# A plain column pair's last products moved behind the next pair's first job, its weights shifted by 192 bytes

## The chip, the cores and the metric

The kernel runs on one core of a Trainium2 chip. The metric is the device time of one execution in microseconds (us); lower is better. The kernel before takes 904.31 us, the median of three runs (903.77 to 905.09). Names of engines: PE is TensorE, DVE is VectorE, ACT is ScalarE, POOL is GpSimd, and SP issues most of the DMAs.

## What is computed

The reference is one layer of an encoder trunk over 512 rows of 1024 channels: a norm, a wide input projection, three mixers (pooling, differential attention, a gated recurrence), gates, an output projection, and then a SwiGLU feed-forward part with a hidden width of 2816. Only the feed-forward input is touched by the change:

```
h2 = rms_norm(x, norm2_g[l])
gu = h2 @ w_ffn_in[l]
x = x + (jax.nn.silu(gu[..., :FFN_HIDDEN]) * gu[..., FFN_HIDDEN:]) @ w_ffn_out[l]
```

All of it is float32 in and out.

## The kernel before

Every float32 operand of a large product is split into a rounded part and the rest, named `hi` and `lo` (`split_w`, L176: ACT casts `hi`, DVE subtracts to get `lo`). A product is then three terms on PE, hi by hi, hi by lo and lo by hi, added up in one PSUM bank. `cols_mm` writes such a product for 8 blocks of 128 input channels, that is 24 matmuls.

The hidden width is cut into 22 column blocks of 128 (j = 0 to 21). Each needs a gate product and an up product, and so the two blocks of weights are called a pair. Pairs 1 to 21 are computed by a Strassen-like scheme in four jobs (`ffn_pair_bodies`, L1117: `first`, `second`, `third`, `fourth`), with matmuls of 256 rows: 24, 24, 24 and 12 of them. It needs sums of weight blocks (`PairChunk.add`, L255: three DVE instructions at L259, L262 and L263, tile `sums`), splits of those (`shi` on ACT L298, `slo` on DVE L300), and sums of activation blocks (`Forms.make`, tiles `fhi` and `flo`). In `third` a DVE instruction at L1154 reads the bank of the x product (`mm`) into `g`, and `fourth` adds into the same bank, so that the first matmul of `fourth` waits for L1154.

Pair 0 is plain: `ffn_start_job` (L1087) computes pair 1's first job, then the gate product g0 of pair 0 (two halves of 256 rows, since the last rows of h2 come late), then its up product u0 with 24 matmuls of 512 rows into a bank named `rc`. After that pair 1's other three jobs follow, then pair 2's four, and so on.

PE takes its matmuls in the order in which the program writes them. The order on DVE and ACT is set by a scheduler at build time, from its own model of time, and can be pinned by `behind(...)`, which places an instruction after given others. Each engine works through its own list in order, and waits on semaphores where it needs another's result.

At j = 4 the first job ends with two matmuls of 512 rows into a bank `tp` that nobody reads. The second one's moving rows start 16 elements, 64 bytes, further than the first one's. The kernel also has paddings of 192 and 64 bytes between tiles. In the built program the h2 and form tiles start 224 bytes past a multiple of 256, and the split weights 32 bytes past one.

Of the kernel before, what the change touches and what calls it, by code (L numbers as in the profile page):

```python
# [18 lines left out]
P = 128  # L19
# [3 lines left out]
KT = D // P  # L23
# [53 lines left out]
def encoder_kernel(ctx: ExitStack, tc: tile.TileContext, x, norm1_g, w_in, pool_w, pool_scale,  # L77
# [11 lines left out]
    def mm(out_, lhsT, rhs, start, stop, chain=False):  # L89
        i = nc.tensor.matmul(out_, lhsT=lhsT, rhs=rhs, start=start, stop=stop, skip_group_check=chain)  # L90
        tc.keep_in_program_order(i)
        n = 1
        for d in rhs.shape[1:]:
            n *= d
        pipe.t += max(0.107, n * 0.0004167 + 0.002) if rhs.dtype == F32R else max(0.216, n * 0.001667 + 0.004)
# [18 lines left out]
    def bank(name, shape=(P, 512)):  # L114
        return psum.tile(list(shape), F32, name=name, bufs=2 if name == "tp" else 3)
# [46 lines left out]
    class Part:  # L162
# [9 lines left out]
        def split(self):  # L172
            self.hi, self.lo = split_w(self.view(self.chunk.raw), self.a, self.b, self.wpool, self.skip)
            self.chunk.left -= 1

    def split_w(view, a, b, wpool=None, skip=0):  # L176

        n, k = a * b, skip // 4
        hi, lo = ((wpool or wsp).tile([P, n if wpool else 1088], F32R, name=name)[:, k:k + n]
                  .rearrange("p (a b) -> p a b", a=a) for name in ("whi", "wlo"))  # L180
        nc.scalar.copy(out=hi, in_=view)  # L181
        nc.vector.tensor_tensor(out=lo, in0=view, in1=hi.bitcast(F32), op=ALU.subtract)  # L182
        return hi, lo
# [46 lines left out]
    jobs = Jobs()  # L230
# [34 lines left out]
    @contextmanager  # L265
    def behind(after):

        with ExitStack() as st:
            for i in after:
                st.enter_context(tc.issue_after(i))  # L270
            yield
# [39 lines left out]
    def pair_parts(name, src1, src2, after=(None,) * 4):  # L311
        ch = PairChunk(src1, src2)
        ch.name = name
        ch.after = after
        return [PairPart(ch, i) for i in range(4)]

    def product(ps, part, n, r, start):

        terms = [(part.hi, r[0]), (part.hi, r[1]), (part.lo, r[0])]
        for i, (w, m) in enumerate(terms):  # L320
            for k in range(KT // 2):
                mm(ps, w[:, n, k, :], m[:, k, :], start and i == 0 and k == 0,
                   i == 2 and k == KT // 2 - 1, True)
                if k % 2:
                    yield
# [73 lines left out]
    def cols_mm(ps, part, r, nk, sub=0, lo_col=0, n=512, r_lo_last=False):  # L399
        c = slice(lo_col, lo_col + n)  # L400
        ws = slice(sub * P, sub * P + P)
        terms = [(part.hi, r[0]), (part.hi, r[1]), (part.lo, r[0])]
        if r_lo_last:
            terms[1:] = terms[:0:-1]
        for i, (w, m) in enumerate(terms):
            for k in range(nk):
                mm(ps[:, c], w[:, k, ws], m[:, k, c], i == 0 and k == 0, i == 2 and k == nk - 1)
                if k % 2:
                    yield
# [51 lines left out]
    hT = (hTp.tile([P, KT, S], F32R, name="hT_hi"), hTp.tile([P, KT, S], F32R, name="hT_lo"))  # L461
# [35 lines left out]
    first = []  # L497
# [513 lines left out]
    OUT = {}  # L1011
# [49 lines left out]
    FF = {}  # L1061
    wf = w_ffn_in[0]

    def ffn_pair_evac(j, pg, pu):
        sl = FF["t"].tile([P, S], F32, name="silu")
        nc.scalar.activation(out=sl, in_=pg, func=AF.Silu)
        nc.vector.tensor_tensor(out=hid_of(j), in0=pu, in1=sl, op=ALU.mult)

    def hid_of(j):
        return FF["hid"][j // 8][:, j % 8, :]  # L1070
# [3 lines left out]
    def hid_split(half, jp):  # L1074

        if (half, jp) in hid_parts:
            return
        early = half == 0 and jp < 2
        hi, lo = ((LAST["ws"] if early else FF["hs"]).tile([P, 2, S], F32R, name=n)
                  for n in (("shi", "slo") if early else ("hhi", "hlo")))  # L1080
        j = 2 * jp
        view = FF["hid"][j // 8][:, j % 8:j % 8 + 2, :]
        nc.scalar.copy(out=hi, in_=view)
        nc.vector.tensor_tensor(out=lo, in0=view, in1=hi.bitcast(F32), op=ALU.subtract)
        hid_parts[half, jp] = hi, lo

    def ffn_start_job(p1, u0, g0):  # L1087


        yield ("e", "H1", 1.3)  # L1090
        yield from pair_bodies[1][0](p1)
        FF["first"] = [bank("mm"), bank("rc")]
        yield from cols_mm(FF["first"][0], g0, OUT["hT"], KT, 0, 0, 256)
        yield ("e", "H3", 1.3)
        yield from cols_mm(FF["first"][0], g0, OUT["hT"], KT, 0, 256, 256, True)
        yield from cols_mm(FF["first"][1], u0, OUT["hT"], KT)

    class TilePart:

# [7 lines left out]
            return True  # L1107

        def split(self):
            self.hi, self.lo = split_w(self.chunk.raw[:, self.c], KT, P)  # L1110
            self.chunk.left -= 1

    def ffn_cols(j):

        return [wf[:, o + j * P:o + (j + 1) * P].rearrange("(kt p) c -> p kt c", p=P) for o in (FFN, 0)]

    def ffn_pair_bodies(j):  # L1117
        c = {}


        def first(part):
            f = FF["forms"]
            c["x"], c["zy"] = bank("mm")[:, 0:256], bank("rc")
            c["u"] = FF["t"].tile([P, S], F32, name="u")
            yield from product(c["x"], part, 0, f.r11, True)
            nc.scalar.copy(out=c["u"][:, 0:256], in_=c["x"])
            yield from product(c["zy"][:, 0:256], part, 1, f.r21, True)


            if j == 4:  # L1130
                w = part.hi.rearrange("p n k c -> p (n k c)")
                for skip in (0, 16):
                    mm(bank("tp"), w[:, 0:P], w[:, skip:skip + 512], True, True)

        def second(part):
            f = FF["forms"]
            y = c["y"] = c["zy"][:, 256:]
            if j == 2:
                with behind(FF["s12_2"]):
                    ffn_pair_evac(0, *FF["first"])  # L1140
            c["g"] = FF["t"].tile([P, S // 2], F32, name="g2")
            yield from product(c["x"], part, 1, f.n2, False)
            nc.scalar.copy(out=c["u"][:, 256:], in_=c["x"])
            yield from product(y, part, 0, f.n1, True)
            FF["y1"] = (nc.scalar.copy(out=c["g"], in_=y).ins,)

        def third(part):
            f = FF["forms"]
            if j == 1:
                with behind(FF["forms_end"]):  # L1150
                    pairs[2][1].chunk.add()
            c["sl"] = FF["t"].tile([P, S], F32, name="silu")
            yield from product(c["x"], part, 0, f.d, False)
            on_dve = nc.vector.tensor_tensor(out=c["g"], in0=c["x"], in1=c["g"], op=ALU.add).ins  # L1154
            if j == 1:
                FF["g1"] = (on_dve,)
            nc.scalar.activation(out=c["sl"][:, 256:], in_=c["g"], func=AF.Silu, scale=-1.0)
            yield from product(c["y"], part, 1, f.r22, False)
            nc.vector.tensor_tensor(out=c["u"], in0=c["u"], in1=c["zy"], op=ALU.add)

        def fourth(part):
            f = FF["forms"]
            yield from product(c["x"], part, 0, f.n4, False)
            nc.scalar.activation(out=c["sl"][:, 0:256], in_=c["x"], func=AF.Silu, scale=-1.0)
            nc.vector.tensor_tensor(out=hid_of(j), in0=c["sl"], in1=c["u"], op=ALU.mult)
            if j == FT - 1:
                for jp in range(2):
                    hid_split(0, jp)

        return first, second, third, fourth  # L1170

    pair_bodies = {j: ffn_pair_bodies(j) for j in range(1, FT)}
    after = {1: (None, None, "forms_mid", "forms_mid"), 2: ("g1",) * 4, 3: ("s12_2",) * 4}
    pairs = {j: pair_parts(j, *ffn_cols(j), after.get(j, (None,) * 4)) for j in range(1, FT)}
    plain = PairChunk(*ffn_cols(0))
    plain.where = "pl"
    u0, g0 = TilePart(plain, 0), TilePart(plain, 1)
    jobs.add([pairs[1][0], u0, g0], ffn_start_job)
    n_out = len(jobs.jobs)
    for j in range(1, FT):  # L1180
        for i in range(0 if j > 1 else 1, 4):
# [193 lines left out]
```

## Time and profile before

| what | value |
|---|---|
| median of three runs | 904.31 us (903.77 to 905.09) |
| the profiled execution | 903.87 us, its span 902.0 us |
| mean granted TensorE clock | 0.998 |
| PE busy | 885.1 us, 98% of the span |
| DVE, ACT busy | 586.3 us (65%), 420.8 us (47%) |
| DMA | 89.00 MB, mean 99 GB/s |

The span is the time from the first to the last instruction; 1.87 us of the execution lie around it. Times inside the trace count from the span's start. In a timeline row the columns are start in us, length in us, engine, line, operation, the names written and read, the shape, and how many instructions the row merges. Matmuls overlap in the pipeline, so a matmul's length says little: the pace is the distance from one start to the next, divided by the count.

### The profile page before, as it was taken

The numbers are of one execution on the slowest core, as the hardware profiler recorded it, in microseconds if no ns is written. First come the engines' busy times: TensorE is split into PE (matmuls) and PEld (weight loads), VectorE is DVE, ScalarE is ACT, GpSimd is POOL, SyncE is SP. The second block draws the span as 40 slices with busy tenths as digits, with TensorE's granted clock in tenths as the row PEclk, the third lists the DMA queues.
The fourth block names the chain that finished last, engine by engine and source line by source line (L and its number), as shares of the span: only waits on it lengthen the run. The fifth ranks groups of instructions, "written<-read, shape, count | busy, mean of one in ns | idle before, by whom it ended". The sixth has DMA issues, their size and how long they took to land.

```text
span 902.0 us, 13155 instructions
## 1 busy us (share of the span) xinstructions
PE 885.1 (98%) x5355; PEld 782.7 (87%) x5355; DVE 586.3 (65%) x904; ACT 420.8 (47%) x652; POOL 19.4 (2%) x34
## 2 busy tenths in 40 slices
PE   6999999999999999999999999999999999999996
PEld 5989978878998888788888898999999999888885
DVE  5787566844859764644425735998888888545544
ACT  5544343424746583332223414756556556434432
POOL 2000000000000000000000001000000000000000
PEclk9999999999999999999999999999999999999999
DMA  8330113024134115422224440154434334323302
GB/s 248 105 117 24 47 48 117 24 71 135 44 94 138 48 47 188 151 94 94 94 94 140 140 118 1 48 140 123 113 94 135 100 98 137 117 70 119 108 31 94
DMA packets 106312, 89.00 MB, mean 99 GB/s; under 512 B 2686, under 2 KB 93324, under 8 KB 106124
## 3 DMA queue, kind: packets, MB, share of 16 engines
q1 hardware_dynamic: 105532, 86.59, 31.2%
q10 hardware_dynamic: 720, 1.57, 0.5%
q8 instruction: 42, 0.69, 0.3%
q14 instruction: 18, 0.15, 0.1%
HBM read 86.06 MB, written 2.10 MB: 98 GB/s over the span
## 4 chain that ended last, share of the span: by engine, by line
PE 94%; DVE 3%; DMA 1%; ACT 1%; issue 1%; POOL 0%; POOLq 0%; SPq 0%; ACTq 0%; DVEq 0%
PE mm L90 66%; PE rc L90 23%; PE tp L90 4%; PE tp L98 2%; DMA xin<-in_x_dram 1%; DVE hid L352 1%; DMA raw<-in_w_ffn_in_dram 0%; DVE flo L352 0%; DVE h_lo L451 0%; DVE wlo L182 0%; DVE slo L300 0%; DVE hrow L432 0%; PE rc L98 0%; ACT x L1218 0%; ACT hrow L426 0%
## 5 line engine op out<-in xcount | busy, mean ns | idle before, releaser
L182 DVE TENSOR_TENSOR wlo<-raw,whi 128x1024 fp32r<-128x1024 f32 (+1 forms) x146 | 166.5, 1144 | 154.9 <-PE mm L90 77.7
L181 ACT CAST whi<-raw 128x1024 fp32r<-128x1024 f32 (+1 forms) x146 | 143.5, 990 | 211.3 <-PE mm L90 126.7
L90 PE MATMUL mm<-hT_hi,whi 128*128 128x512 f32 (+1 forms) x440 | 111.8, 390 | 0.0
L90 PE MATMUL mm<-hT_hi,wlo 128*128 128x512 f32 (+1 forms) x440 | 108.1, 381 | 0.0
L90 PE MATMUL mm<-hT_lo,whi 128*128 128x512 f32 (+1 forms) x440 | 107.9, 382 | 0.0
L90 PEld LDWEIGHTS mm<-hT_hi,whi 128*128 128x128 f32 x440 | 79.2, 191 | 16.9 <-issue 2.9
L90 PEld LDWEIGHTS mm<-hT_lo,whi 128*128 128x128 f32 x440 | 79.0, 188 | 14.8
L90 PEld LDWEIGHTS mm<-hT_hi,wlo 128*128 128x128 f32 x440 | 78.9, 188 | 14.6
L300 DVE TENSOR_TENSOR slo<-sums,shi 128x1024 fp32r<-128x1024 f32 x42 | 51.1, 1218 | 0.0
L298 ACT CAST shi<-sums 128x1024 fp32r<-128x1024 f32 x42 | 44.2, 1053 | 2.2 <-DVE sums L262 1.8
L763 DVE TENSOR_TENSOR kq<-kq,pyr 128x256 f32<-128x256 f32 x56 | 21.5, 420 | 25.6 <-PE rc L90 25.5
L90 PEld LDWEIGHTS rc<-kq,kc 128*128 128x128 f32 x224 | 30.3, 191 | 2.1 <-issue 0.5
L90 PE MATMUL rc<-kq,kc 128*128 128x128 f32 x224 | 31.6, 284 | 0.0
L885 ACT ACTIVATE s<-s,mx 128x512 f32<-128x512 f32 x32 | 23.1, 721 | 15.5 <-DVE mx L883 15.4
L727 ACT COPY kc<-kq 128x512 f32<-128x512 f32 x28 | 18.6, 666 | 21.8 <-PE rc L90 15.6
L90 PE MATMUL mm<-fhi,slo 128*128 128x256 f32 x168 | 26.1, 277 | 0.5 <-DVE slo L300 0.4
L90 PE MATMUL mm<-y_hi,whi 128*128 128x512 f32 x96 | 26.4, 393 | 0.0
L90 PE MATMUL mm<-y_lo,whi 128*128 128x512 f32 x96 | 26.2, 392 | 0.0
L90 PE MATMUL mm<-fhi,shi 128*128 128x256 f32 x168 | 26.0, 277 | 0.1
L90 PE MATMUL mm<-y_hi,wlo 128*128 128x512 f32 x96 | 25.9, 390 | 0.0
L90 PE MATMUL mm<-flo,shi 128*128 128x256 f32 x168 | 25.9, 276 | 0.0
L90 PE MATMUL mm<-whi,hhi 128*128 128x512 f32 x66 | 25.7, 389 | 0.0
(254 smaller groups left out, 1787.9 us busy)
## 6 DMA issues: line engine op xcount, KB each, us to landing
raw<-in_w_ffn_in_dram SPq DMA_DIRECT2D x44, 512.0 KB, 5.3
raw<-in_w_in_dram SPq DMA_DIRECT2D x18, 1024.0 KB, 5.2
raw<-in_w_in_dram SPq DMA_DIRECT2D x24, 512.0 KB, 4.1
raw<-in_w_ffn_out_dram SPq DMA_DIRECT2D x10, 1024.0 KB, 5.1
raw<-in_w_out_dram SPq DMA_DIRECT2D x4, 1024.0 KB, 5.2
xin<-in_x_dram SPq DMA_DIRECT2D x4, 512.0 KB, 9.4
raw<-in_w_up_rec_dram SPq DMA_DIRECT2D x2, 1024.0 KB, 7.8
x<-in_x_dram SPq DMA_DIRECT2D x1, 2048.0 KB
```

What stands on the lines that cost most here:

```text
L90: i = nc.tensor.matmul(out_, lhsT=lhsT, rhs=rhs, start=start, stop=stop, skip_group_check=chain)
L98: tc.keep_in_program_order(nc.tensor.transpose(out_, in_, idn))
L181: nc.scalar.copy(out=hi, in_=view)
L182: nc.vector.tensor_tensor(out=lo, in0=view, in1=hi.bitcast(F32), op=ALU.subtract)
L298: nc.scalar.copy(out=hi, in_=view)
L300: on_dve = nc.vector.tensor_tensor(out=lo, in0=view, in1=hi.bitcast(F32), op=ALU.subtract).ins
L352: last[0] = form(**kw).ins
L727: nc.scalar.copy(out=strided(kc, 0, [[2 * n, S // (2 * n)], [n, 2], [1, n]]), in_=strided(kq, 2 * S, [[2 * n, S // (2 * n)], [S + n, 2], [ ...
L763: nc.vector.tensor_tensor(out=xv, in0=xv, in1=tv, op=ALU.mult)
L885: nc.scalar.activation(out=s, in_=s, func=AF.Exp, scale=-1.0, bias=mx[:, c:c + 1], accum_out=zz[:, i, c:c + 1])
```

## The change

There are five edits. The order of the two plain products' parts becomes g0, u0 in the job's list. u0's 24 products are cut into three terms of eight; the first two terms stay where they were, and the third (u0's `lo` part) is written at the end of pair 2's first job. One matmul that nobody reads follows it, with u0's first `lo` block as stationary part and pair 2's `hi` weights from element 16 as moving part; the two at j = 4 are gone. The split weights of both g0 and u0 lie 192 bytes further in their tiles, so that they start 224 bytes past a multiple of 256. And the three DVE instructions that add up pair 2's weight blocks are placed behind pair 1's L1154 (L1162 in the new file), no longer ahead of it.

```
-        yield from cols_mm(FF["first"][1], u0, OUT["hT"], KT)
+        yield from first_u(u0, 0)
+        yield from first_u(u0, 1)
+        FF["u0"] = u0
+
+    def first_u(u0, term):
+        w, m = (u0.lo if term == 2 else u0.hi), OUT["hT"][term % 2]
+        for k in range(KT):
+            mm(FF["first"][1], w[:, k, :], m[:, k, :], (term, k) == (0, 0), (term, k) == (2, KT - 1), True)
+            if k % 2:
+                yield
...
-            self.hi, self.lo = split_w(self.chunk.raw[:, self.c], KT, P)
+            self.hi, self.lo = split_w(self.chunk.raw[:, self.c], KT, P, None, 192)
...
-            if j == 4:
+            if j == 2:
+                yield from first_u(FF["u0"], 2)
                 w = part.hi.rearrange("p n k c -> p (n k c)")
-                for skip in (0, 16):
-                    mm(bank("tp"), w[:, 0:P], w[:, skip:skip + 512], True, True)
+                mm(bank("tp"), FF["u0"].lo[:, 0, :], w[:, 16:528], True, True)
...
-            if j == 1:
-                with behind(FF["forms_end"]):
-                    pairs[2][1].chunk.add()
...
             if j == 1:
                 FF["g1"] = (on_dve,)
+                with behind(FF["g1"]):
+                    pairs[2][1].chunk.add()
```

Where the instructions now stand is shown at three places. The numbers behind names are those of one tile; `x4` merges four instructions.

PE, around the end of pair 2's first job (tiles `mm_4994` and `rc_4995`, after the change `mm_4986` and `rc_4987`), before:

```order
L90 MATMUL rc_4995<-h2_hi_4263,whi_4961 128x256 x4
L90 MATMUL rc_4995<-h2_lo_4264,whi_4961 128x256 x4
L90 MATMUL rc_4995<-h2_hi_4263,wlo_4962 128x256 x4
L90 MATMUL mm_4994<-fhi_4866,shi_4965 128x256 x4
L90 MATMUL mm_4994<-flo_4867,shi_4965 128x256 x4
```

The same place after the change, where `rc_4760` is u0's bank and `wlo_4536` its `lo` weights:

```order
L90 MATMUL rc_4987<-h2_hi_4263,wlo_4954 128x256 x4
L90 MATMUL rc_4760<-h2_hi_4263,wlo_4536 128x512 x8
L90 MATMUL tp_5022<-whi_4953,wlo_4536 128x512
L90 MATMUL mm_4986<-fhi_4858,shi_4957 128x256 x4
L90 MATMUL mm_4986<-flo_4859,shi_4957 128x256 x4
```

Eight matmuls and one now stand between pair 2's first and second job; the eight are gone from the end of u0, ahead of pair 1's second job.

DVE, around pair 1's reading of its x bank (`g2`), before:

```order
L352 TENSOR_TENSOR flo_4867<-hid2_4861,fhi_4866 128x1024
L259 TENSOR_TENSOR sums_4929<-raw_4420 128x2x512
L1154 TENSOR_TENSOR g2_4902<-mm_4731,g2_4902 128x256
L182 TENSOR_TENSOR wlo_4962<-raw_4420,whi_4961 128x1024
L182 TENSOR_TENSOR wlo_4988<-raw_4420,whi_4987 128x512
L1159 TENSOR_TENSOR u_4733<-u_4733,rc_4732 128x512
L262 TENSOR_TENSOR sums_4929<-sums_4929,raw_4420 128x512
```

After the change:

```order
L352 TENSOR_TENSOR flo_4859<-hid2_4853,fhi_4858 128x1024
L1162 TENSOR_TENSOR g2_4894<-mm_4731,g2_4894 128x256
L259 TENSOR_TENSOR sums_4935<-raw_4420 128x2x512
L182 TENSOR_TENSOR wlo_4954<-raw_4420,whi_4953 128x1024
L1169 TENSOR_TENSOR u_4733<-u_4733,rc_4732 128x512
L262 TENSOR_TENSOR sums_4935<-sums_4935,raw_4420 128x512
L182 TENSOR_TENSOR wlo_4980<-raw_4420,whi_4979 128x512
```

The reading of the x bank moved ahead of the first sum, and one `lo` split of 512 moved behind two others.

DVE, a little later, around the split that pair 2's third job needs (`slo_4971`, now `slo_4963`), before:

```order
L1067 TENSOR_TENSOR hid2_4880<-rc_4760,silu_5026 128x512
L182 TENSOR_TENSOR wlo_5111<-raw_4899,whi_5110 128x512
L300 TENSOR_TENSOR slo_4971<-sums_4929,shi_4969 128x1024
L259 TENSOR_TENSOR sums_5056<-raw_4899 128x2x512
L1154 TENSOR_TENSOR g2_5029<-mm_4994,g2_5029 128x256
```

After the change:

```order
L1067 TENSOR_TENSOR hid2_4872<-rc_4760,silu_5028 128x512
L300 TENSOR_TENSOR slo_4963<-sums_4935,shi_4961 128x1024
L182 TENSOR_TENSOR wlo_5113<-raw_4891,whi_5112 128x512
L259 TENSOR_TENSOR sums_5058<-raw_4891 128x2x512
L1162 TENSOR_TENSOR g2_5031<-mm_4986,g2_5031 128x256
```

The split of pair 2 moved one place forward, ahead of a split for pair 3; the reading of pair 2's x bank keeps its place.

More of the change, by code (lines that the diff above doesn't have):

```diff
@@ L1085, in hid_split, with ffn_start_job @@
         hid_parts[half, jp] = hi, lo
-    def ffn_start_job(p1, u0, g0):
+    def ffn_start_job(p1, g0, u0):
         yield ("e", "H1", 1.3)
@@ L1177, in encoder_kernel @@
     u0, g0 = TilePart(plain, 0), TilePart(plain, 1)
-    jobs.add([pairs[1][0], u0, g0], ffn_start_job)
+    jobs.add([pairs[1][0], g0, u0], ffn_start_job)
     n_out = len(jobs.jobs)
```

## The prediction

> **What bounds the kernel now.** I read the page first, then the PE timeline of the feed-forward input, and then DVE's timeline beside it. From the page, the busy times and the chain of work that ended last:
>
> ```profile
> PE 885.1 (98%) x5355; PEld 782.7 (87%) x5355; DVE 586.3 (65%) x904; ACT 420.8 (47%) x652; POOL 19.4 (2%) x34
> PE 94%; DVE 3%; DMA 1%; ACT 1%; issue 1%; POOL 0%; POOLq 0%; SPq 0%; ACTq 0%; DVEq 0%
> ```
>
> PE is the bound, with 94% of the chain. So only two things can move the time: gaps between matmuls, and the pace of the matmuls. The windows view gives the pace of three long stretches (length, then PE's busy time and count):
>
> ```profile
> 390.00:512.00 122.00, 122.00 (x540) 101.03 (x539) 51.29 (x59) 37.97 (x46) 0.00 (x0) 1.00 0.34 112
> 513.00:535.60 22.60, 22.60 (x193) 22.56 (x193) 11.07 (x17) 5.95 (x8) 0.00 (x0) 1.00 0.60 163
> 606.00:774.00 168.00, 168.00 (x1484) 168.00 (x1484) 141.72 (x175) 97.52 (x159) 0.00 (x0) 1.00 0.41 113
> ```
>
> The first is 512 rows at 122.00/540 = 0.226 us a matmul. The last two are 256 rows at the same granted clock of 1.00, and yet 22.60/193 = 0.117 and 168.00/1484 = 0.113. The feed-forward input already runs at the faster pace without a gap from 606 us to its end, so there is nothing to win there and something to lose. What can be won lies between 569 and 606 us. PE there:
>
> ```profile
> 562.90 1.07 PE L90 MATMUL mm<-h_hi,whi 128*128 128x256 f32 x8
> 563.81 1.07 PE L90 MATMUL mm<-h_lo,whi 128*128 128x256 f32 x8
> ...
> 569.37 2.02 PE L90 MATMUL rc<-h_hi,whi 128*128 128x512 f32 x8
> 571.23 2.03 PE L90 MATMUL rc<-h_lo,whi 128*128 128x512 f32 x8
> ...
> 579.96 0.62 PE L90 MATMUL rc<-h_hi,slo 128*128 128x256 f32 x4
> 580.66 0.73 PE L90 MATMUL mm<-fhi,whi 128*128 128x256 f32 x4
> 581.24 0.62 PE L90 MATMUL mm<-flo,whi 128*128 128x256 f32 x4
> ...
> 584.41 0.62 PE L90 MATMUL rc<-h_hi,wlo 128*128 128x256 f32 x4
> 585.08 0.72 PE L90 MATMUL mm<-fhi,shi 128*128 128x256 f32 x4
> 585.64 0.62 PE L90 MATMUL mm<-flo,shi 128*128 128x256 f32 x4
> 586.34 0.74 PE L90 MATMUL mm<-fhi,slo 128*128 128x256 f32 x4
> 586.92 0.63 PE L90 MATMUL rc<-fhi,shi 128*128 128x256 f32 x4
> ...
> 588.80 0.63 PE L90 MATMUL mm<-flo,shi 128*128 128x256 f32 x4
> 589.81 0.74 PE L90 MATMUL mm<-fhi,slo 128*128 128x256 f32 x4 [0.38 <-DVE slo L300]
> 590.39 0.62 PE L90 MATMUL rc<-h_hi,shi 128*128 128x256 f32 x4
> ...
> 591.75 0.50 PE L90 MATMUL mm<-fhi,whi 128*128 128x256 f32 x3
> ...
> 605.35 0.63 PE L90 MATMUL tp<-whi 128*128 128x512 f32 x2
> 605.81 0.63 PE L90 MATMUL mm<-fhi,shi 128*128 128x256 f32 x4
> ```
>
> From 590.39 to 605.35 stand 132 matmuls, 14.96/132 = 0.1133 each, 0.453 for four. Four waits show as longer steps: 579.96 to 580.66, 584.41 to 585.08, 585.64 to 586.34, 588.80 to 589.81. In each the four matmuls behind the wait also take 0.56 to 0.58, so a wait costs its idle time and about 0.11 more. Both together, the four waste 0.37, 0.32, 0.37 and 0.68 us, about 1.75. And after the third wait the pace is 0.1175 (586.92 to 588.80, 16 matmuls), although the same operands run at 0.1133 otherwise: PE has two paces at these addresses, and a wait can leave it in either. DVE in the same stretch:
>
> ```profile
> 576.19 1.22 DVE L300 TENSOR_TENSOR slo<-sums,shi 128x1024 fp32r<-128x1024 f32 x1
> ...
> 579.06 1.22 DVE L259 TENSOR_TENSOR sums<-raw 128x1024 f32<-128x1024 f32 x1
> 580.19 0.42 DVE L1154 TENSOR_TENSOR g<-mm,g 128x256 f32<-128x256 f32 x1
> 580.53 1.81 DVE L182 TENSOR_TENSOR wlo<-raw,whi 128x1024 fp32r<-128x1024 f32 x2
> ...
> 583.84 0.69 DVE L1165 TENSOR_TENSOR hid<-silu,u 128x512 f32<-128x512 f32 x1 [0.29 <-ACT silu L1164]
> 585.06 1.23 DVE L300 TENSOR_TENSOR slo<-sums,shi 128x1024 fp32r<-128x1024 f32 x1
> ...
> 587.94 0.68 DVE L182 TENSOR_TENSOR wlo<-raw,whi 128x512 fp32r<-128x512 f32 x1
> 588.54 1.22 DVE L300 TENSOR_TENSOR slo<-sums,shi 128x1024 fp32r<-128x1024 f32 x1
> 589.79 1.23 DVE L259 TENSOR_TENSOR sums<-raw 128x1024 f32<-128x1024 f32 x1
> 590.94 0.41 DVE L1154 TENSOR_TENSOR g<-mm,g 128x256 f32<-128x256 f32 x1
> ```
>
> Each wait ends 0.05 us after a DVE instruction: 580.61 (L1154) and 580.66, 586.29 (slo) and 586.34, 589.76 (slo) and 589.81. So DVE's list is what PE runs against here, and DVE's list has hardly a gap. A wait is taken by the weight load, which starts with the matmul ahead of it; so a result must be there 0.05 + 0.11 us ahead of its matmul.
>
> **The 192 bytes.** u0's matmuls take (571.23 - 569.37)/8 = 0.2325 us, with moving rows at byte 224 of 256 and weights at 32; the 512-row stretch above, with both at the same remainder, takes 0.226. u0 will have both at 224, so I take 0.227 (bounds 0.226 and 0.2325). The Trainium skill speaks against this edit: "SBUF — State Buffer", section "Who interferes with whom", gives PE two independent read ports, one for the moving operand and one for weight loads, and says that PE never waits on anyone. By it the shift is worth nothing, u0's last eight would stay at 0.2325, and the sum below would be 0.05 us worse. The trace doesn't bear that out, since it has two paces at one shape and clock. The same shift goes to g0, 48 matmuls of 256 rows, now (563.81 - 562.90)/8 = 0.114. The nearest rows with 256 rows and equal remainders:
>
> ```profile
> 25.32 1.12 PE L90 MATMUL mm<-hT_lo,whi 128*128 128x256 f32 x8
> 26.29 1.12 PE L90 MATMUL mm<-hT_hi,wlo 128*128 128x256 f32 x8
> ```
>
> That is 0.97/8 = 0.121, so g0 may lose up to 48 x 0.007 = 0.33 us, at least 0. I take the whole, being the row with like addresses. Twenty of the 48 stand ahead of the last transposes, from which DVE's list goes on; so DVE's list shifts by up to 20 x 0.007 = 0.14, and I add 0.13 to all DVE times.
>
> **The move, step by step.** g0 ends at 569.37 + 0.33 = 569.70. u0's sixteen take 3.63, pair 1's second job 24 x 0.1133 = 2.72; the third job then wants its slo for matmul nine at 576.05 + 0.91 = 576.96. It comes at 577.41 + 0.13 + 0.05 = 577.59: a new wait of 0.63 and 0.11, where none was, because PE arrives earlier. It swallows what the two stretches ahead of it won or lost. From there four matmuls 0.58 and twelve 1.36 give 579.53. L1154 now stands where L259 stood, 579.06 + 0.13, and ends at 579.61; the fourth job starts at 579.66, a wait of 0.13 and 0.11 instead of the first one before. Twelve matmuls, 0.58 + 0.91, give 581.15. Pair 2's first job takes 2.72 to 583.87; its wlo (580.53 + 0.13 + 0.05 and a length of 1.22, as L259 of the same size, is 581.93) is wanted by the weight load at 581.95, just in time. u0's eight take 1.81, to 585.68, and the unread one 0.23, to 585.91. What waits behind these on PE is only pair 2's second job; L1067, which reads u0's bank, stands right ahead of the DVE row at 587.94 and so starts at about 587.3, after the bank is done. One split on ACT, of pair 3's weights, waits for the unread one too, since that reads the tile to be filled; its result is used in pair 3's fourth job, 132 matmuls later.
>
> Pair 2's second job wants slo for a weight load at 585.91 + 0.91 - 0.11 = 586.71; it comes at 586.29 + 0.13 + 0.05 = 586.47 (its place is set by the silu that L1165 waits for at 583.84). No wait. The third job wants its slo at 589.43; that slo now takes the place at 587.94, and comes at 587.94 + 1.22 + 0.18 = 589.34. No wait. The fourth job wants L1154 by 591.24. That stands behind slo, the wlo of 512 and L259: with steps of 1.13 (579.06 to 580.19) and 0.60 (587.94 to 588.54) it starts at 587.94 + 1.13 + 0.60 + 1.13 = 590.80 and ends at 591.21, 591.39 with the 0.18. So one wait, a start at 591.39 and 0.11 behind it, 591.50; before, the same matmul starts at 591.75. **Gain here: 0.25 us.** Four waits gave way to three, two of them new in size.
>
> At j = 4 the unread two go: 605.81 - 605.35 = **0.46**. The sum is 0.71 us, 0.08%. The profiled execution took 903.87 us (its span 902.0 and 1.87 around it), 0.44 under the median of 904.31. By its own time 903.2 follows; from the median, **903.6 us**. About 0.2%, 1.8 us, is what a measurement here can tell from no change.
>
> **The rivals.** *A, the slower pace sticks (910.3 us).* The last wait, at pair 2's fourth job, comes after the unread matmul, and nothing behind it disturbs PE until 774 us; the pair at 605.35 that stood there is gone. If that wait leaves PE in the slower pace, 12 + 19 x 84 = 1608 matmuls take 0.0042 us more each, 6.7 us. That the slower pace can last is shown by 513.00:535.60 above, a whole stage in it (its moving rows start at 32, its weights at 96 bytes past a multiple of 256). Whether a wait leaves it in it: of the four above, one did (586.34) and three did not (580.66, 585.08, 589.81). In the recurrence stage it changes from one resumption to the next:
>
> ```profile
> 93.04 1.07 PE L90 MATMUL mm<-whi,hT_lo 128*128 128x256 f32 x8
> 93.94 1.07 PE L90 MATMUL mm<-wlo,hT_hi 128*128 128x256 f32 x8
> ...
> 96.68 1.10 PE L90 MATMUL mm<-whi,hT_lo 128*128 128x256 f32 x8
> 97.62 1.10 PE L90 MATMUL mm<-wlo,hT_hi 128*128 128x256 f32 x8
> ```
>
> 0.90/8 = 0.1125 and 0.94/8 = 0.1175. It decides at 591.24: if L1154 ends by then, there is no wait, and the pace is the one that the unread matmul leaves; after 605.35 that was the faster within four matmuls. By the two ports of that page of the Trainium skill this rival could not exist at all. I give it 24 in 100, near the one in four.
>
> *B, no gain (904.3 us).* The near-ties at pair 2's first and third job (0.02 and 0.09 us spare) fall the wrong way, each for some 0.15, and pair 2 runs at the slower pace (48 x 0.0042 = 0.2). For it speaks how thin they are, against it that a later PE then finds L1154 done. 12 in 100.
>
> *C, all gaps vanish (902.1 us).* All 1.75 us of waits and the 0.46 go, and no new wait comes, which would need the one at 577.59 not to be; DVE's list up to there is untouched, so I give it 3 in 100.
>
> **How the numbers follow.** The forecast (a gain of 0.5 to 1.0 us; 1.0 if g0 keeps its pace and the last wait goes) has 61, A 24, B 12, C 3. Forecast and B lie within 0.2%; A is slower, C faster. So faster 0.03, same 0.73, slower 0.24. The forecast's own range is 902.9 to 904.5: the bounds, and half of the spread of the runs before. With A more than 2 in 10 would be left out, so the range reaches up to it: 902.8 to 910.6.
>
> **What would show it.** In the profile after: the u0 rows at 0.227; g0's at 0.121 or 0.114; a step near 577.6 in pair 1's third job; no wait in pair 2's second and third job; a short one at its fourth; and the feed-forward input's rows of four at 0.453 apart (then the time is 903 to 904) or 0.47 apart (then about 910). The forecast is wrong if a wait longer than 0.5 us stands after 584 us, or the pace differs.

## The result, and the profile after

The changed kernel takes 910.38 us (median of four executions, 910.09 to 911.27) against 904.70 us (903.77 to 905.37) before: a ratio of 1.0061, 95% interval 1.0032 to 1.009. It is slower by 5.7 us; the forecast was 903.6 us, a gain of 0.7. The profiled execution took 910.09 us, its span 908.3 us, 6.3 more than before, at a granted clock of 0.997. Several kernels of this study, the kernel before among them, come out near 904 in some executions and near 911 in others, at the same granted clock, and how many of each is part of what was measured.

The page's busy times:

```profile
PE 891.6 (98%) x5354; PEld 789.8 (87%) x5354; DVE 586.4 (65%) x904; ACT 421.5 (46%) x652; POOL 19.4 (2%) x34
```

PE is busy 6.5 us longer with one matmul less, while DVE and ACT have the same work as before. So it is pace, not gaps. The windows view (length, then PE's busy time and count) over the stretch that was shown of before:

```profile
606.00:774.00 168.00, 168.00 (x1429) 168.00 (x1428) 138.25 (x170) 93.51 (x153) 0.00 (x0) 1.00 0.39 107
```

There were 1484 matmuls in it, 0.1132 us each; now there are 1429, 0.1176 each, at the same clock of 1.00, with not a gap in either. Rival A's outcome has come. Where it begins is seen in PE's timeline:

```profile
562.65 1.12 PE L90 MATMUL mm<-h_hi,whi 128*128 128x256 f32 x8
563.61 1.12 PE L90 MATMUL mm<-h_lo,whi 128*128 128x256 f32 x8
...
569.31 2.00 PE L90 MATMUL rc<-h_hi,whi 128*128 128x512 f32 x8
571.15 1.98 PE L90 MATMUL rc<-h_lo,whi 128*128 128x512 f32 x8
572.97 0.63 PE L90 MATMUL mm<-fhi,shi 128*128 128x256 f32 x4
573.44 0.64 PE L90 MATMUL mm<-flo,shi 128*128 128x256 f32 x4
...
576.43 0.62 PE L90 MATMUL mm<-flo,shi 128*128 128x256 f32 x4
577.32 0.74 PE L90 MATMUL mm<-fhi,slo 128*128 128x256 f32 x4 [0.27 <-DVE slo L300]
577.90 0.62 PE L90 MATMUL rc<-h_hi,shi 128*128 128x256 f32 x4
578.35 0.62 PE L90 MATMUL rc<-h_lo,shi 128*128 128x256 f32 x4
578.81 0.62 PE L90 MATMUL rc<-h_hi,slo 128*128 128x256 f32 x4
579.39 0.72 PE L90 MATMUL mm<-fhi,whi 128*128 128x256 f32 x4
...
583.14 2.46 PE L90 MATMUL rc<-h_hi,wlo 128*128 128x256 f32 x12
585.43 0.40 PE L90 MATMUL tp<-whi,wlo 128*128 128x512 f32 x1
585.67 0.64 PE L90 MATMUL mm<-fhi,shi 128*128 128x256 f32 x4
586.14 0.63 PE L90 MATMUL mm<-flo,shi 128*128 128x256 f32 x4
...
590.85 0.63 PE L90 MATMUL rc<-h_hi,slo 128*128 128x256 f32 x4
591.32 0.64 PE L90 MATMUL mm<-fhi,whi 128*128 128x256 f32 x4
591.79 0.64 PE L90 MATMUL mm<-flo,whi 128*128 128x256 f32 x4
```

The row at 583.14 merges pair 2's last four products with u0's last eight, which are 512 rows wide. Twice the slower pace, 0.47 for four, begins with no wait ahead: at 572.97 behind u0's first sixteen, and at 585.67 behind its last eight and the unread one. The first time the waits in pair 1 end it (0.45 from 577.90 to 578.81). The second time nothing does. No wait stands at 591.32, where the forecast and rival A both had one, and from 585.67 to the stage's end 19 x 84 + 60 = 1656 matmuls run 0.0044 us slower each: 7.3 us. That is the 6.3, and about 1.0 less elsewhere. Of this 1.0, 0.25 was there ahead of the first product that the change touches: g0 starts at 562.65, against 562.90 before.

### The profile page after: what moved, and what is told of

Read it like the earlier page. It is cut to its first block, busy times and chain, and to the rows that moved or that the text cites. A ratio compares the mean times of both kernels' runs of the same rounds, so it can differ in the third digit from the quotient of the medians.

```text
span 908.3 us, 13154 instructions
## 1 busy us (share of the span) xinstructions
PE 891.6 (98%) x5354; PEld 789.8 (87%) x5354; DVE 586.4 (65%) x904; ACT 421.5 (46%) x652; POOL 19.4 (2%) x34
## 5 line engine op out<-in xcount | busy, mean ns | idle before, releaser
L300 DVE TENSOR_TENSOR slo<-sums,shi 128x1024 fp32r<-128x1024 f32 x42 | 51.1, 1218 | 0.0
L298 ACT CAST shi<-sums 128x1024 fp32r<-128x1024 f32 x42 | 44.2, 1053 | 2.7 <-DVE sums L262 1.5
L1162 DVE TENSOR_TENSOR g<-mm,g 128x256 f32<-128x256 f32 x21 | 8.9, 424 | 27.9 <-PE mm L90 26.3
```

What stands on the lines that cost most here:

```text
L300: on_dve = nc.vector.tensor_tensor(out=lo, in0=view, in1=hi.bitcast(F32), op=ALU.subtract).ins
```

## The experiments

Theories are named as their expectations name them. "Addresses" means the start of the moving rows and of the weights past a multiple of 256 bytes, written 224/32 for 224 and 32. All matmuls of 256 rows behind u0 in the feed-forward input are 224/32. A step is the time from one matmul's start to the next one's.

**Two unread matmuls put back (e1_pair_back).** The edit, to the kernel after:

```
+            if j == 4:
+                w = part.hi.rearrange("p n k c -> p (n k c)")
+                for skip in (0, 16):
+                    mm(bank("tp"), w[:, 0:P], w[:, skip:skip + 512], True, True)
```

> The kernel after, with the two unread matmuls of j = 4 put back (moving rows at byte 32 and 96, weights at 32 of 256). Theory H (the last 512-row matmul ahead of a stretch of 256-row matmuls hands its phase over by the addresses that it reads, and nothing but a wait or another 512-row matmul changes it): 0.1176 us a matmul from 585.7 to about 606, then 0.1133; the 1484 matmuls behind win 1484 x 0.0044 = 6.5 us and the pair costs 0.46, so about 904.3 us. Rival T (the slower pace comes from something else that the change altered for good, such as DVE's order or where tiles lie): 0.1176 stays to the end, 910.9 us.

Measured: 911.13 us (910.74 to 911.54). Theory H falls as it was put. Rival T's time came, but DVE's order is not the cause: e7 and e10 below have one order and differ. The timeline of that kernel around the pair:

```profile
605.54 0.64 PE L90 MATMUL rc<-h_lo,whi 128*128 128x256 f32 x4
606.01 0.64 PE L90 MATMUL rc<-h_hi,wlo 128*128 128x256 f32 x4
606.48 0.62 PE L90 MATMUL tp<-whi 128*128 128x512 f32 x2
606.95 0.63 PE L90 MATMUL mm<-fhi,shi 128*128 128x256 f32 x4
607.41 0.63 PE L90 MATMUL mm<-flo,shi 128*128 128x256 f32 x4
607.88 0.63 PE L90 MATMUL mm<-fhi,slo 128*128 128x256 f32 x4
608.36 0.64 PE L90 MATMUL rc<-fhi,shi 128*128 128x256 f32 x4
```

0.47 for four ahead of the pair and 0.47 behind it. The pair hands on the pace that it met; at 605.35 in the kernel before it had met the faster one. It resets nothing.

**Without the 192 bytes (e2_no_shift).**

```
-            self.hi, self.lo = split_w(self.chunk.raw[:, self.c], KT, P, None, 192)
+            self.hi, self.lo = split_w(self.chunk.raw[:, self.c], KT, P)
```

> The kernel after without the 192 bytes: the weights of g0 and u0 lie at byte 32 of 256 again, so that the unread matmul reads moving rows at 96 and weights at 32. Same instructions in the same order. Theory H: as behind the pair at 605.35 before, 0.1133 from the unread matmul on; 910.4 less 1655 x 0.0044 = 7.3, less 48 x 0.006 = 0.3 for g0, plus 24 x 0.006 = 0.15 for u0, so about 903.0 us. Rival M (the move of the eight matmuls or the missing pair is what leaves the slower pace, whatever the addresses): 910.3 us.

Measured: 910.13 us (909.76 to 910.29), 0.1176 from 585.73 on. H missed again, and rival M's time came; but e7 below keeps the move, lacks the pair as well, and is fast. This run holds a clue: at 573.00, behind u0's first sixteen alone (now 224/32), 0.1133 followed at once, without a wait. Behind the same class of matmuls and the unread one at 96/32 the slower pace followed. Taking the shift away is not enough while the single unread matmul stands there.

**The unread matmul with other weights (e5_own_weights).**

```
-                mm(bank("tp"), FF["u0"].lo[:, 0, :], w[:, 16:528], True, True)
+                mm(bank("tp"), w[:, 0:P], w[:, 16:528], True, True)
```

> The kernel after with one operand of the unread matmul changed: its stationary block is pair 2's first hi block (byte 32), not u0's lo block (byte 224); u0 keeps its 192 bytes. Theory H, with the last matmul deciding alone: 0.1133 from 585.7 on, 910.4 less 7.3, so about 903.1 us. Rival S (the state is set by u0's eight at 224 and 224, and one matmul behind them can't change it): 0.1176, 910.4 us.

Measured: 910.42 us (909.77 to 911.61); 0.1176 from 585.71 on. As S expected, but e2 has the slower pace without any eight at 224/224.

**Without any unread matmul (e3_no_unread).** The two lines that write it are deleted.

> The kernel after without any unread matmul: u0's last eight (moving rows and weights both at byte 224) stand directly ahead of pair 2's second job. Theory H: as at 572.97 in the kernel after, where u0's first sixteen end, the slower pace follows, 910.2 us. Rival U (the unread matmul itself, with moving rows at 96 and weights at 224, is what sets it): 0.1133 from 585.5 on, about 902.9 us.

Measured: ten executions, seven from 902.63 to 903.08 and three from 909.92 to 911.08. Neither theory had that. PE's timeline of a profiled execution of 903.08 us:

```profile
585.47 0.63 PE L90 MATMUL mm<-fhi,shi 128*128 128x256 f32 x4
585.94 0.63 PE L90 MATMUL mm<-flo,shi 128*128 128x256 f32 x4
...
588.76 0.64 PE L90 MATMUL mm<-flo,shi 128*128 128x256 f32 x4
589.53 0.74 PE L90 MATMUL mm<-fhi,slo 128*128 128x256 f32 x4
590.11 0.62 PE L90 MATMUL rc<-h_hi,shi 128*128 128x256 f32 x4
590.57 0.62 PE L90 MATMUL rc<-h_lo,shi 128*128 128x256 f32 x4
```

The slower pace starts at 585.47, as H had it, but a wait at 589.53 ends it: without the unread matmul PE comes earlier, and the scheduler at build time also put this slo one place later on DVE. So a wait sets the pace anew, and not always to the faster one. The kernel before does it too: over the study's 97 executions of it, 74 came out near 904 and 23 near 911. From here on theory P, as the next expectations put it, replaced H: the pace is a phase that one matmul hands to the next.

**Without the shift and without an unread matmul (e6_no_shift_no_unread).** The edits of e2 and e3 together.

> The kernel after without the 192 bytes and without any unread matmul. Theory P (PE's pace is a phase that one matmul hands to the next; a run of 512-row matmuls settles it by its addresses and its last member, a wait sets it anew by chance, anything else leaves it): u0's last eight, moving rows at 224 and weights at 32 and ending on a step of 236 ns, are what stood ahead of 574.97 in the kernel before, so 0.1133 from 585.5 on. A wait of about 0.4 us follows at pair 2's third job and throws the pace anew, fast in about 3 of 4 executions: 902.9 us in those, 910 in the others. Rival D (behind u0's eight at this place the slower pace comes whatever the addresses, by what DVE and the DMAs do then): 0.1177 from 585.5 to the wait.

Measured: ten of twelve executions from 902.66 to 903.69, two at 909.85 and 909.95. In the profile u0's last eight end on a step of 235 ns, and from 585.09 the steps are 119, 113, 113, 114: the faster pace at once, at the very place. Rival D falls. Then a wait of 0.63 us, which ends at 589.35, throws the pace anew, as forecast, longer than the 0.4 expected.

**A wait added to the kernel after (e8_late_read).**

```
             yield from product(c["x"], part, 0, f.d, False)
+            if j == 2:
+                nc.vector.tensor_tensor(out=c["sl"][:, 0:256], in0=c["x"], in1=c["g"], op=ALU.add)
             on_dve = nc.vector.tensor_tensor(out=c["g"], in0=c["x"], in1=c["g"], op=ALU.add).ins
```

> The kernel after with one more DVE instruction in pair 2's third job, which reads the x bank as L1162 does and writes a tile that is overwritten later; the scheduler puts it and L262 ahead of L1162, about 1.0 us. Theory P: slower pace from 585.7 as before, then a new wait of 0.5 us and 0.11 at pair 2's fourth job (591.3), which sets the pace anew: in about 3 of 4 executions 0.1133 from there on, 910.4 - 1608 x 0.0044 + 0.6 = 904.0 us, in the others 911.0. Rival R (waits have nothing to do with it: what the unread matmul and u0 left stays): 911.0 in all.

Measured: nine of twelve executions from 903.25 to 904.61, three from 910.46 to 911.36. PE around the new wait, in an execution of 903.89 us:

```profile
590.69 0.64 PE L90 MATMUL rc<-h_lo,shi 128*128 128x256 f32 x4
591.16 0.63 PE L90 MATMUL rc<-h_hi,slo 128*128 128x256 f32 x4
592.13 0.74 PE L90 MATMUL mm<-fhi,whi 128*128 128x256 f32 x4 [0.34 <-DVE g L1164]
592.72 0.62 PE L90 MATMUL mm<-flo,whi 128*128 128x256 f32 x4
593.17 0.62 PE L90 MATMUL mm<-fhi,wlo 128*128 128x256 f32 x4
593.62 0.62 PE L90 MATMUL mm<-h_hi,whi 128*128 128x256 f32 x4
```

0.47 before the wait, 0.45 behind it: more work on DVE and a wait on PE make the changed kernel about 6.5 us faster in three executions of four (903.89, the middle of the nine, against 910.38; the chips differ). That is the size and the share that P gave; rival R falls.

**The kernel before without its pair (e4_before_no_pair).**

```
-            if j == 4:
-                w = part.hi.rearrange("p n k c -> p (n k c)")
-                for skip in (0, 16):
-                    mm(bank("tp"), w[:, 0:P], w[:, skip:skip + 512], True, True)
```

> The kernel before without the two unread matmuls of j = 4. Theory P: they only preserve the pace that they meet, so that 0.46 us are won and the share of slow executions stays as it was (about 1 in 7): 903.5 us, with some at 910. Rival Q (the pair is what resets a slower pace in the kernel before): the pace of the wait at 589.81 lasts, and about 1 in 4 executions is slow.

Measured: eight of twelve from 902.82 to 904.36 (median 903.63, against 903.99 for the lower group of the kernel before beside it, so about 0.4 won of the 0.46), four from 910.13 to 911.4. Four of twelve against eight of 35 of the kernel before beside it is too few to tell P from Q; e1 tells it.

**Two unread matmuls alike (e7_two_alike).** To e2's kernel:

```
-                w = part.hi.rearrange("p n k c -> p (n k c)")
-                mm(bank("tp"), FF["u0"].lo[:, 0, :], w[:, 16:528], True, True)
+                for k in (6, 7):
+                    mm(bank("tp"), FF["u0"].lo[:, k, :], OUT["hT"][0][:, k, :], True, True)
```

> The kernel after without the 192 bytes, and with two unread matmuls in place of the one: repeats of u0's last two, with moving rows at 224 and weights at 32 (ending on a step of 236 ns again). Theory P: 0.1133 from about 586 on; the 0.47 us of the two make PE come 0.1 to 0.3 us later to pair 2's third job than without them, so that there is a wait of 0.1 us at most or none. Without a wait every execution is fast: 903.0 us (902.6 to 903.4). Rival D: the slower pace from 586 to the end, 910.4.

Measured: all twelve executions from 902.95 to 903.77, median 903.18; the ratio to the kernel before, over all executions of both, is 0.9972, interval 0.995 to 0.9993. The timeline and the window:

```profile
585.85 0.63 PE L90 MATMUL tp<-h_hi,wlo 128*128 128x512 f32 x2
586.32 0.62 PE L90 MATMUL mm<-fhi,shi 128*128 128x256 f32 x4
586.78 0.62 PE L90 MATMUL mm<-flo,shi 128*128 128x256 f32 x4
587.23 0.62 PE L90 MATMUL mm<-fhi,slo 128*128 128x256 f32 x4
...
606.00:774.00 168.00, 168.00 (x1484) 168.00 (x1484) 142.18 (x175) 97.20 (x159) 0.00 (x0) 1.00 0.40 114
```

0.455 for four from the first one on, no wait behind, and 1484 matmuls in the window.

**The same with the 192 bytes (e10_two_shifted).** The 192 of e2's edit put back. Each engine's instructions stand in the same order as in e7; only u0's and g0's weights lie elsewhere.

> The kernel e7 with the 192 bytes back on u0 and g0, as in the kernel after; every engine's list is the same word for word, so that it differs from e7 in addresses alone. The ten matmuls of 512 rows then have moving rows and weights both at 224 and settle at 227 ns. Theory P: as in all runs where such matmuls stand ahead (572.97 and 585.67 in the kernel after), 0.1177 from about 586.1 to the end, about 910.5 us in every execution. Rival W (what made e7 fast is its two alike matmuls, or the 0.47 us by which they delay PE, and not the addresses): 0.1133, 903.2 us.

Measured: all twelve from 910.39 to 911.2, median 910.98:

```profile
586.30 0.61 PE L90 MATMUL tp<-h_hi,wlo 128*128 128x512 f32 x2
586.75 0.63 PE L90 MATMUL mm<-fhi,shi 128*128 128x256 f32 x4
587.22 0.64 PE L90 MATMUL mm<-flo,shi 128*128 128x256 f32 x4
587.69 0.63 PE L90 MATMUL mm<-fhi,slo 128*128 128x256 f32 x4
...
606.00:774.00 168.00, 168.00 (x1428) 168.00 (x1428) 138.81 (x172) 93.80 (x153) 0.00 (x0) 1.00 0.39 109
```

The ten matmuls themselves are the faster ones, 227 ns against 233, and all 1656 behind them the slower ones. Addresses alone make 7.8 us between e7's median and e10's, of which up to about 1 may be the difference between two chips (the lower group of the kernel before had medians of 903.99 and 904.94 beside them). The Trainium skill's "SBUF — State Buffer", section "Who interferes with whom", gives PE's two reads independent ports and says nothing of their addresses; in these two kernels the addresses mattered by that much.

**Three alike (e9_three_alike).** `(5, 6, 7)` for `(6, 7)` in e7.

> The kernel e7 with three unread matmuls alike in place of two; DVE's list is the same word for word. In e7 the ten matmuls took 231 and 236 ns in turn and ended on 236, and 0.1133 followed; at 573.03 of the same run the sixteen of u0 ended on 231, and 0.118 followed. Theory P (the last member of the 512-row run hands over the pace): the eleven end on 231, 0.1177 from 586.6 to the end, with no wait that could change it: 903.2 + 0.23 + 1655 x 0.0044 = 910.7 us in every execution. Rival A (the addresses alone decide, 224 and 32 being good): 0.1133, 903.4 us.

Measured: ten of eleven executions from 911.21 to 912.08, one at 904.05. As P expected, but for the one, and the test wasn't clean: bank `tp` has two tiles, the third matmul waited for PE's own first write, and its step was 322 ns. The next two mend that.

**Three, and four, into one bank (e11_three_one_bank, e12_four_one_bank).** To e7's kernel:

```
+                tp = bank("tp")
-                for k in (6, 7):
-                    mm(bank("tp"), FF["u0"].lo[:, k, :], OUT["hT"][0][:, k, :], True, True)
+                for k in (5, 6, 7):
+                    mm(tp, FF["u0"].lo[:, k, :], OUT["hT"][0][:, k, :], True, True)
```

and `(4, 5, 6, 7)` in the other.

> As e9, but the three unread matmuls write one and the same bank. In e9 each took a new tile of two that are there, so that the third had to wait for PE's own first write (a last step of 322 ns); here no wait stands between u0's eight and pair 2's second job, and DVE's list is that of e7. Theory P (the last member of the 512-row run hands over the pace): steps of 231 and 236 in turn over eleven, the last 231, then 0.1177 to the end in every execution: e7's 903.2 + 0.23 + 7.3 = 910.7 us on a chip where before takes 904.0. Rival A (224 and 32 are good addresses, whatever the last member, and e9's wait was what made it slow): 0.1133, 903.4 us.

> As e11 with four unread matmuls. Theory P: twelve steps in turn, the last 236, then 0.1133 from 586.8 on; nothing waits behind it, so every execution takes e7's 903.2 + 0.47 = 903.7 us on a chip where before takes 904.0. Rival N (the count doesn't matter; more unread matmuls or a later PE bring the slower pace): 0.1177, 911 us. Rival A of e11 gives 903.7 too.

Measured: with three, all twelve from 910.71 to 911.84; with four, all twelve from 903.2 to 904.69 (median 903.88, ratio 0.9966, interval 0.9939 to 0.9994). One more matmul whose result nobody reads, the same operands, and 7 us. The windows of the two, three first:

```profile
606.00:774.00 168.00, 168.00 (x1429) 168.00 (x1428) 138.75 (x171) 93.41 (x153) 0.00 (x0) 1.00 0.39 110
```

```profile
606.00:774.00 168.00, 168.00 (x1485) 168.00 (x1484) 141.84 (x175) 96.65 (x158) 0.00 (x0) 1.00 0.40 112
```

Rivals A and N fall. Ten handovers from 512 to 256 rows without a wait between, as single steps (ns from one matmul's start to the next) in the profiled executions:

```
kernel, at     512-row addresses       their last steps      first 256-row steps   pace after
before 574.97  224/32                  231 236 231 236       118 113 114           0.1133
e7     573.26  224/32                  236 230 236 231       118 118 117           0.1177
e6     585.09  224/32                  231 236 231 235       119 113 113           0.1133
e7     586.32  224/32                  230 236 231 236       118 114 113           0.1133
e11    587.00  224/32                  236 231 236 230       119 117 118           0.1177
e12    587.64  224/32                  234 233 233 234       121 116 114           0.1133
after  572.97  224/224                 226 227 227 226       118 117 118           0.1177
e10    586.75  224/224                 226 227 227 226       118 117 118           0.1177
after  585.67  224/224, then 96/224    227 226 227 233       120 118 117           0.1177
e2     585.73  224/32, then 96/32      235 231 236 228       116 118 118           0.1177
```

At 224/32 the steps go 231 and 236 in turn, and what follows goes by the last: 236 or 235 the faster pace, 231 or 230 the slower. There is a third way, even steps of 233 (e12's profiled execution, and e4 at 574.61), which also gave the faster pace; why it was even there, the runs don't say, and in these executions it was not the last step's turn that decided. At 224/224, 227 each, the slower pace followed every time. The fifteen other handovers of u0's matmuls without a wait in the fourteen traces fit the same pattern. The pairs at j = 4 do not: behind these two matmuls, at 32/32 and 96/32, the faster pace followed a last step of 232 (before), and the slower one a step of 236 (e1).

## Why the prediction was wrong, point by point

- **The 192 bytes: price right, effect missed.** u0 runs at (571.15 - 569.31)/8 = 0.230 and then (572.97 - 571.15)/8 = 0.2275, against the 0.227 taken; g0 at (563.61 - 562.65)/8 = 0.120 against 0.121. The whole of g0 took 0.19 us longer than before, where 0.33 was taken. But the edit was priced by its own 72 matmuls alone. What it can do to the matmuls behind is some 7 us, not tenths: e10 against e7. In the changed kernel itself it is one of two causes, since the single unread matmul left the slower pace without it too (e2).
- **The new wait in pair 1: right in kind.** Forecast at 577.59, measured at 577.32; the fourth job was forecast at 579.66 and started at 579.39. A short extra one at 575.86 (its step is 0.07 longer) was not forecast. The 0.27 has one reason: DVE's list came 0.14 earlier than in the profile before (L300 at 576.05, against 576.19), and the forecast took it 0.13 later; this fits PE's lead of 0.25 at g0.
- **Pair 2's second and third job without a wait: right.** The unread matmul was forecast to end at 585.91; 585.67. One reading of the prediction is wrong here: of the four waits before, the one that ended at 585.08 was for ACT's `shi` (L298, done at 585.03), not for DVE, and the working has no term for it. It did no harm: that `shi` was done at 584.53 after.
- **The wait at pair 2's fourth job: forecast, and it didn't come.** L1154 (now L1162) was to end at 591.21, 591.39 with the 0.18. DVE after:

```profile
583.35 0.69 DVE L1175 TENSOR_TENSOR hid<-silu,u 128x512 f32<-128x512 f32 x1
...
590.31 0.42 DVE L1162 TENSOR_TENSOR g<-mm,g 128x256 f32<-128x256 f32 x1
```

  It ends at 590.73. The forecast held L1165 (now L1175) at 583.84 + 0.13 because a silu releases it. L1175 starts at 583.35, 0.62 earlier than taken, and so does all behind it. The silu does release it, but what sets the silu is on ACT, and the forecast has no term for it: it stands behind a cast of pair 3's weights, which waits for their DMA. ACT before, and after:

```profile
582.47 1.05 ACT L181 CAST whi<-raw 128x1024 fp32r<-128x1024 f32 x1 [0.92 <-DMA raw<-in_w_ffn_in_dram]
583.43 0.38 ACT L1164 ACTIVATE silu<-mm 128x256 f32<-128x256 f32 x1
```

```profile
581.99 1.06 ACT L181 CAST whi<-raw 128x1024 fp32r<-128x1024 f32 x1 [1.71 <-DMA raw<-in_w_ffn_in_dram]
582.94 0.38 ACT L1174 ACTIVATE silu<-mm 128x256 f32<-128x256 f32 x1
```

  That DMA was issued at 578.03 before and at 577.90 after; from issue to cast it took 4.44 and 4.09 us. So 0.35 of the 0.62 is the DMA's, and 0.27 is the shift of DVE's list named above. From issue to cast the fourteen profiled executions show 3.93 to 4.50, so luck has a part in it: by an estimate from these rows, with 4.44 L1162 would have ended at 591.08, only 0.08 ahead of what the matmul at 591.32 needs.
- **The step that failed: the pace behind the unread matmul.** The prediction named the case, "if L1154 ends by then, there is no wait, and the pace is the one that the unread matmul leaves", and then took the faster, because that followed within four matmuls after 605.35. That pair had met the faster pace and had other addresses (32/32 and 96/32) than the single one (96/224), which stands behind u0's 224/224. The pair hands the pace on (e1). The change's matmuls set the slower one, in all four executions by their times, and each part of them is enough: without the shift the slower pace still came behind the unread matmul, there at 96/32 (e2), and without the unread matmul u0's eight at 224/224 did, until a wait ended it (e3).
- **Rival A: size right, place and chance wrong.** 910.3 us was its time, 910.38 the result, and the stated range holds the result only because it was stretched up to this rival. That the two are so close is in part luck: A counted 1608 matmuls at 0.0042, 6.7 us, where 1656 at 0.0044, 7.3 us, were lost. It was to come by a wait leaving the slower pace, one time in four. That share is about right for waits: in the 14 profiled executions, 36 of the 47 waits of pairs 1 and 2 left the faster pace and 11 the slower. But here no wait stood behind the handover, and then it isn't a chance.
- **The sum of 0.71 us: right in size, as far as the pace lets it be seen.** Pair 2's fourth job starts at 591.32 against 591.75, 0.43 earlier (0.25 forecast). Of this, 0.25 was there before g0 began, ahead of the moved products; on the other side the 48 matmuls of pair 2's second and third job lost 48 x 0.0044 = 0.21 by the slower pace. At the faster one it would be about 0.39, an estimate from these rows, and 0.46 is the pair. e7, which has the same moves, no shift and one unread matmul more, has a median 0.81 below the lower group of the kernel before (903.18 against 903.99).

What stays open: why PE has the two paces, and what in a wait picks one. No experiment looked inside. That the 23 executions of the kernel before near 911 are ones in which its last wait, at 589.81, left the slower pace fits their distance of about 7 us (1624 matmuls from there to the stage's end, times 0.0044, is 7.1), but none of them has a trace.

## What to carry to other kernels

Where a long stretch of matmuls runs without a wait, look at what stands directly ahead of it: on the trace, read the pace in its first dozen steps and at its end, and count a change of operand addresses, or of the number of matmuls ahead, by all that the stretch holds. If one kernel's executions fall in two groups at the same granted clock, compare the groups and not the medians, and look for the last wait ahead of the longest stretch. The version that beats both kernels here (e7: the moves kept, the shift dropped, two unread matmuls alike) wins 0.8 us by its moves, and more by having all its executions in the lower group: its mean is 903.31 us, against 905.67 for the 35 of the kernel before beside it.

## What the runs showed of the hardware

- 256-row matmuls with moving rows at 224 and weights at 32 past a multiple of 256 bytes have two lasting paces at the same granted clock of 1.00: 0.1133 us (steps of 113, 113, 114 ns) and 0.1177 (117 to 119). Either lasted over 1400 matmuls.
- A 512-row matmul's own pace and the pace that it leaves are different things: 224/224 is the faster class (227 ns against 233) and with or without one unread matmul behind it left the slower pace, by their times, in all 24 executions of the kernels in which no wait followed (the kernel after, e1, e5, e10).
- A wait on PE costs its idle time and about 0.11 us: in each of the 47 waits the first step behind it took 0.221 to 0.229 us in place of 0.113 or 0.118. It also sets the pace anew, which was worth about 6.5 us in e8.
